# Feed-forward stages of a decoder layer: a first pair of chunks in seven block products

## The chip, the core and the metric

One core of a Trainium2 chip runs the whole layer as one program. The metric is the device time of one execution in microseconds (us). A change of 0.2% is 3.9 us here.

## The reference

A layer for 256 tokens of width 2048, everything in float32: a half-step SwiGLU feed-forward stage, a token mixer with two attention branches, and a second feed-forward stage, each followed by a LayerNorm on the residual sum.

```python
def _swiglu(x, w_gate, w_up, w_down):
    return (jax.nn.silu(x @ w_gate) * (x @ w_up)) @ w_down
...
h = _layer_norm(ALPHA * h + 0.5 * _swiglu(h, ffn1_w_gate[l], ffn1_w_up[l], ffn1_w_down[l]), ln1_g[l], ln1_b[l])
mix = _mixer(h, ...)
h = _layer_norm(ALPHA * h + mix, ln2_g[l], ln2_b[l])
h = _layer_norm(ALPHA * h + 0.5 * _swiglu(h, ffn2_w_gate[l], ffn2_w_up[l], ffn2_w_down[l]), ln3_g[l], ln3_b[l])
```

The gate and up matrices are 2048 x 5632 each. The change lies in `x @ w_gate` and `x @ w_up` of both feed-forward stages, in their first 512 columns of each matrix.

## The kernel before, in words

**Numbers in two parts.** Every float32 operand is split into a high part (a cast on ACT, L154) and a low part (source minus high part, on DVE, L155). A product is three matmuls (`triple`, L208 to L210): high x high, high x weights' low, low x weights' high. Each moves 512 columns. So no weight reaches TensorE before ACT and then DVE have gone over it. The two parts of a block of weights stand in a pair of tiles, `wring`, out of a ring of 10 pairs at first and of 6 in the steady state: this is how far ACT and DVE can work ahead of TensorE.

**Tiles and chunks.** The 256 tokens are two halves, b = 0 and 1. The 2048 rows of weights are 16 k tiles of 128; x is kept turned, in four quads of 4 k tiles (quad 0 holds k tiles 0 to 3). Gate and up are cut into 22 chunks of 512 columns (256 of gate, 256 of up). A unit is two k tiles of a chunk, one load of 512 KB: `raw` (4 buffers) when it is used once, `sraw` when it stays for several uses.

**Plain units and seven products.** `project` does a chunk plainly: 8 units, each used for both token halves, 12 matmuls a unit. `Hybrid.group` does a pair of chunks together. It takes the two token halves, the two chunks and two groups of k tiles as a 2 x 2 block product in Winograd's form, with seven products (forms 1 to 7, two units of 6 matmuls each) where eight would be needed. This holds for k tiles 0 to 7; the rest of the pair is plain. The weights' sums that the forms need are made in place in `sraw` blocks, by adds on DVE (L430) and by accumulating loads that POOL issues (L432). The sums of x are made once a stage by `Seven` (`fa`, `fb` at L289, split into `xs`; the negated quad at L313) and `Extra` (`fe`, `xe`, `xm`; L329, L341). The order of forms and plain units is a string (`"15pp6p7p2q4q3qq"`: digits are forms, p and q plain units of the first and second chunk).

**The opening of a stage.** Chunks 0 and 1 are done by `project`, one after the other: 16 units, 192 matmuls. x arrives quad by quad meanwhile: in the first stage by loads (`load_x`, L1453 to L1456), in the second from LayerNorm's rows, normalised (L895), transposed on TensorE (L673) and scaled (L680, L681 or ACT L685). The second token half's products run up to five units behind the first's (`lag`), since its x comes later. From chunks 2 and 3 on, the groups run; the first of them starts its banks unseeded, the later ones seeded (`begin`). In the second stage the blocks 11, 12 and 22 of the first group are loaded ahead, during chunk 1 (L979).

**Order.** Each engine runs its own queue in order. The order is fixed when the program is built: `later` puts a step some units on, `tc.issue_after` keeps an instruction behind another. Finished banks are taken by `half`: Silu on ACT (L914), product on DVE (L921, `hb`), turning (L717, `blocks`) and a store. A group's banks are first joined with a sum that was kept in SBUF (L940, `gus`; `snap` by ACT).

## Time and profile before

| what | us |
|---|---|
| three timed runs | 1965.83, 1966.58, 1967.08 |
| median | 1966.58 |
| span of the profiled execution, first to last instruction | 1963.9 |
| PE busy in it | 1952.0 |
| DVE busy | 1779.9 |
| ACT busy | 1251.5 |
| first stage's opening (first product to the first group) | about 5 to 50 |
| second stage's opening | about 1274 to 1318 |

The timed runs give the whole execution and the profile gives its span; about 2.7 us of the median lie outside the span. A row of a timeline has start, length, engine, line, operation, what it writes and reads, and in brackets the idle time ahead of it with what ended it. Overlapping instructions of an engine are pipelined: the distance of two starts is then the cost of one, not its length.

### The profile page before, as it was taken

How to read it: one execution, taken by the hardware profiler on the slowest of the kernel's cores; microseconds unless marked ns; L12 is line 12 of the kernel's file. 1: busy time of each engine (PE TensorE's matmuls, PEld its weight loads, DVE VectorE, ACT ScalarE, POOL GpSimd, SP SyncE). 2: the span in 40 equal slices, each digit the busy share in tenths (PEclk: the TensorE clock that was granted, in tenths of full speed). 3: DMA queues.
4: the chain of work that ended last, by engine and by line, in shares of the span. 5: the costliest groups of instructions: out<-in, count | busy, mean ns of one | idle time of the engine just before them, and what ended most of it. 6: DMA issues, size and time to landing. Idle time of an engine off the chain costs nothing.

```text
span 1963.9 us, 25802 instructions
## 1 busy us (share of the span) xinstructions
PE 1952.0 (99%) x8763; PEld 1617.7 (82%) x8763; DVE 1779.9 (91%) x2189; ACT 1251.5 (64%) x1640; POOL 312.1 (16%) x536
## 2 busy tenths in 40 slices
PE   9999999999999999999999999999999999999998
PEld 7888888888888898888788888888888888888886
DVE  7999999999998879988987777789999999999997
ACT  6666766676655566666667655556676666665662
POOL 0112111122100010102241530001211112210000
PEclk9999999999999999999999999999999999999999
DMA  8978888878776667767685798587888878787773
GB/s 314 289 225 262 270 260 249 257 233 300 272 235 222 210 216 258 239 223 252 211 254 195 237 305 271 201 264 254 252 269 263 250 240 277 241 318 236 277 232 124
DMA packets 150228, 488.86 MB, mean 249 GB/s; under 512 B 21792, under 2 KB 22096, under 8 KB 150096
## 3 DMA queue, kind: packets, MB, share of 16 engines
q1 hardware_dynamic: 119232, 401.00, 59.7%
q0 software_dynamic: 30720, 86.09, 16.8%
q8 instruction: 68, 1.11, 0.2%
q14 instruction: 64, 0.52, 0.1%
q10 hardware_dynamic: 144, 0.13, 0.0%
HBM read 456.73 MB, written 30.41 MB: 248 GB/s over the span
## 4 chain that ended last, share of the span: by engine, by line
PE 95%; DVE 2%; DMA 1%; issue 1%; ACT 0%; POOL 0%; SPq 0%; DVEq 0%; ACTq 0%; POOLq 0%
PE mm L208 30%; PE mm L210 30%; PE mm L209 30%; DVE wring L155 1%; PE tr L208 1%; PE tr L210 1%; PE tr L209 1%; PE tr L673 0%; DMA turned<-turn 0%; ACT wring L154 0%; DMA sraw<-in_wdk_dram 0%; DVE sraw L430 0%; PE tr L1376 0%; PE tr L1304 0%; PE tr L1378 0%
## 5 line engine op out<-in xcount | busy, mean ns | idle before, releaser
L154 ACT CAST wring<-raw 128x1024 fp32r<-128x1024 f32 (+2 forms) x468 | 482.7, 1035 | 323.5 <-PE mm L210 237.6
L155 DVE TENSOR_TENSOR wring<-raw,wring 128x1024 fp32r<-128x1024 f32 (+2 forms) x468 | 557.0, 1198 | 95.6 <-ACT wring L154 93.5
L154 ACT CAST wring<-sraw 128x1024 fp32r<-128x1024 f32 x436 | 453.1, 1052 | 201.7 <-DVE sraw L430 83.6
L155 DVE TENSOR_TENSOR wring<-sraw,wring 128x1024 fp32r<-128x1024 f32 x436 | 520.3, 1218 | 20.6 <-ACT wring L154 17.8
L208 PE MATMUL mm<-wring,h 128*128 128x512 f32 (+2 forms) x1248 | 480.9, 385 | 0.1
L210 PE MATMUL mm<-wring,h 128*128 128x512 f32 (+2 forms) x1248 | 480.3, 385 | 0.0
L209 PE MATMUL mm<-wring,h 128*128 128x512 f32 (+2 forms) x1248 | 479.9, 385 | 0.0
L208 PE MATMUL mm<-wring,xs 128*128 128x512 f32 x776 | 302.2, 389 | 0.5 <-ACT snap L387 0.5
L209 PE MATMUL mm<-wring,xs 128*128 128x512 f32 x776 | 302.1, 389 | 0.0
L210 PE MATMUL mm<-wring,xs 128*128 128x512 f32 x776 | 301.9, 389 | 0.0
L210 PEld LDWEIGHTS mm<-wring,h 128*128 128x128 f32 x1248 | 234.4, 188 | 47.0 <-DVE h L155 0.7
L208 PEld LDWEIGHTS mm<-wring,h 128*128 128x128 f32 x1248 | 234.4, 188 | 46.7 <-ACT h L154 0.6
L209 PEld LDWEIGHTS mm<-wring,h 128*128 128x128 f32 x1248 | 234.4, 188 | 46.1
L430 DVE TENSOR_TENSOR sraw<-sraw,sraw 128x1024 f32<-128x1024 f32 x168 | 199.1, 1217 | 2.0 <-DMA sraw<-in_wdk_dram 1.6
L208 PEld LDWEIGHTS mm<-wring,xs 128*128 128x128 f32 x776 | 145.6, 188 | 31.0 <-ACT snap L387 0.9
L209 PEld LDWEIGHTS mm<-wring,xs 128*128 128x128 f32 x776 | 145.7, 188 | 30.5 <-DVE wring L155 0.3
L210 PEld LDWEIGHTS mm<-wring,xs 128*128 128x128 f32 x776 | 145.7, 188 | 30.2
L719 POOL DMA_DIRECT2D hT<-blocks x176 | 96.8, 563 | 368.3 <-DVE blocks L717 367.2
L209 PE MATMUL mm<-wring,x 128*128 128x512 f32 x336 | 130.9, 390 | 0.2 <-DVE wring L155 0.2
L208 PE MATMUL mm<-wring,x 128*128 128x512 f32 x336 | 130.1, 390 | 0.8 <-ACT wring L154 0.8
L210 PE MATMUL mm<-wring,x 128*128 128x512 f32 x336 | 130.7, 389 | 0.0
L432 POOL DMA_DIRECT2D sraw<-in_gu_dram x40 | 35.6, 892 | 371.4 <-DVE sraw L430 334.5
(328 smaller groups left out, 2292.4 us busy)
## 6 DMA issues: line engine op xcount, KB each, us to landing
sraw<-in_gu_dram SPq DMA_DIRECT2D x160, 512.0 KB, 5.2
raw<-in_gu_dram SPq DMA_DIRECT2D x158, 512.0 KB, 5.0
raw<-in_dn_dram SPq DMA_DIRECT2D x140, 512.0 KB, 4.7
sraw<-in_gu_dram POOLq DMA_DIRECT2D x40, 512.0 KB, 7.5
sraw<-in_dn_dram SPq DMA_DIRECT2D x36, 512.0 KB, 5.4
eraw<-in_gu_dram SPq DMA_DIRECT2D x64, 256.0 KB, 5.8
raw<-in_w_out_dram SPq DMA_DIRECT2D x32, 512.0 KB, 4.3
hraw<-hT POOLq DMA_DIRECT2D x56, 256.0 KB, 5.9
```

The source lines that it names most:

```text
L154: cast[0] = S.copy(hi, src)
L155: lows[0] = V.tensor_tensor(out=lo, in0=src, in1=hi.bitcast(F32), op=ALU.subtract)
L208: PE.matmul(o, xh, wh, start=first, stop=False, skip_group_check=again)
L209: PE.matmul(o, xh, wl, start=False, stop=False, skip_group_check=again)
L210: PE.matmul(o, xl, wh, start=False, stop=last, skip_group_check=again)
L430: last = V.tensor_tensor(out=R[src][i], in0=R[src][i], in1=R[add[1]][i], op=ALU.add)
L432: nc.gpsimd.dma_start(R["12"][s], source("22", s), accum_op=ALU.add)
L719: nc.gpsimd.dma_start(to.rearrange("(g r) (i f) -> i r g f", g=4, i=4)[i], t[32 * i:32 * (i + 1), :].rearrange("r (g f) -> r g f", g=4))
```

## The change

Chunks 0 and 1 are now a pair too, in a new method `Hybrid.opening`, with the order `"pqpq1pq536qp742"`. K tiles 8 to 15 (quads 2 and 3) are plain and come first, 8 units of 12 matmuls. K tiles 0 to 7 (quads 0 and 1) are the block product, 14 units of 6 matmuls. So the opening has 22 units and 180 matmuls where it had 16 units and 192. x comes in the order of quads 2, 3, 0, 1, and quads 0 and 1 are no longer split for themselves (`formed`), only their sums are. Form 4 reads the block that forms 1, 5 and 6 have turned into a sum; two of the sums are made by accumulating loads on POOL (after form 1 and after form 6, two loads each), two by adds on DVE. The first group after it is seeded, and the loads ahead of the second stage are gone. The cut diff (in the order's rows below and in the new program all lines are shifted: L155 is L159, L430 is L565 in a group and L438 in the opening, L940 is L1069, L921 is L1056, L895 is L1030):

```diff
@@ class Acts
+            self.formed = formed
+            self.quads = [q for q in range(4) if q not in formed] + list(formed)
...
         def put(self, q, b, src, i0=0, n=4):
+            if q in self.formed:
+                return
@@ class Seven
+            self.opened = [self.minus] + self.steps[:4]
@@ class Hybrid
+        def opening(self, w0, w1, done, order, hook, guard, settle):
...
+            left = {b: 5 for b in "YWZX"}
+            blocks = {"11": (w0, 0), "21": (w0, 2), "22": (w1, 2)}
+            plan = {1: ("11", "11", None, "A"), 5: (None, "11", None, "D"), 6: (None, "11", "22", "A"),
+                    7: (None, "22", None, "A"), 2: ("21", "21", None, "Y"), 4: (None, "11", "21", "W"),
+                    3: ("22", "22", None, "Z")}
...
+                    done(n, m, banks[b], snap[key], op)
+            def plus(key, other):
+                V.tensor_tensor(out=snap[key], in0=snap[key], in1=snap[other], op=ALU.add)
...
+            def seventh(u, p, s):
...
+                    if add is not None:
+                        with behind_split(s + 1):
+                            last = V.tensor_tensor(out=t, in0=t, in1=R[add][s], op=ALU.add)
+                    pair = next_pair()
+                    with guard(u), tc.issue_after(last.ins) if last is not None else nullcontext():
+                        split_in_line(True, *pair, t)
+                    if p in (1, 6):
+                        nc.gpsimd.dma_start(R["11" if p == 1 else "22"][s], w1[s], accum_op=ALU.add)
...
@@ class LayerNorm
-            for c in range(4):
+            for c in self.x.quads:
@@ def ffn
-        project(wgu[0], x, KD, 512, lambda b, bank: gu_done(0, b, bank), hook=first_hook,
-                between=between, norm=norm)
-        project(wgu[1], x, KD, 512, lambda b, bank: gu_done(1, b, bank), hook=second, norm=norm, free=(0, 0))
-        look(3, 4)
-        hy = Hybrid(x, seven, KD, extra=extra, early=early)
+        formed = dict(zip((7, 9, 11, 13, 15, 18) if alone else (4, 8, 11, 13, 15, 18), seven.opened + [extra.make]))
+        hy.opening(wgu[0], wgu[1], lambda n, b, bank, snap, op: sum_done(n, b, bank, snap, op), "pqpq1pq536qp742",
+                   first, guard, settle)
+        hy.widened()
...
-                     1 < p < KF // 4 - 1, p > 1)
+                     1 < p < KF // 4 - 1, True)
@@ the loads of x in the first stage
-    def first_tokens(j):
-        if j % 2 == 0:
-            load_x(j // 2, 0)
-
-    def second_tokens(j):
-        if j % 2 == 0:
-            load_x(j // 2, 1)
+    def tokens(u, late):
+        for q, b in {(0, 0): ((2, 0),), (0, 1): ((2, 1),), (3, 0): ((0, 0),), (4, 0): ((3, 0),), (5, 0): ((3, 1),),
+                     (6, 0): ((0, 1), (1, 0), (1, 1))}.get((u, late), ()):
+            load_x(q, b)
```

**DVE, end of the first stage's opening.** The row before, from the last plain splits of chunk 1 (`raw_415` and on) over the first group's form 1 (`sraw_463`, `sraw_464`) to form 5 (the two L430 adds and the split behind them):

```order
L155 TENSOR_TENSOR wring_115<-raw_415,wring_114 128x1024
L155 TENSOR_TENSOR wring_105<-raw_431,wring_104 128x1024
L313 SCALAR_TENSOR_TENSOR xs_441<-xraw_123,xs_441 128x512
L155 TENSOR_TENSOR wring_103<-raw_444,wring_102 128x1024
L155 TENSOR_TENSOR wring_121<-sraw_463,wring_120 128x1024
L155 TENSOR_TENSOR wring_119<-sraw_464,wring_118 128x1024
L155 TENSOR_TENSOR wring_117<-raw_477,wring_116 128x1024
L430 TENSOR_TENSOR sraw_463<-sraw_463,sraw_465 128x1024
L430 TENSOR_TENSOR sraw_464<-sraw_464,sraw_466 128x1024
L155 TENSOR_TENSOR wring_115<-sraw_463,wring_114 128x1024
```

And now, from the last split of the opening (form 2's second unit) over form 1 (`wring_105`, `wring_103` from `sraw_214`, `sraw_215`) to the split of form 5 (`wring_121`) in the first group:

```order
L159 TENSOR_TENSOR wring_115<-sraw_375,wring_114 128x1024
L411 TENSOR_TENSOR snap_275<-snap_275,snap_274 128x512
L1069 TENSOR_TENSOR gus_449<-mm_169,snap_275 128x512
L159 TENSOR_TENSOR wring_105<-sraw_214,wring_104 128x1024
L1056 TENSOR_TENSOR hb_453<-gus_449,sg_451 128x256
L1069 TENSOR_TENSOR gus_474<-mm_148,snap_274 128x512
L159 TENSOR_TENSOR wring_103<-sraw_215,wring_102 128x1024
L1056 TENSOR_TENSOR hb_453<-gus_474,sg_476 128x256
L565 TENSOR_TENSOR sraw_214<-sraw_214,sraw_404 128x1024
L565 TENSOR_TENSOR sraw_215<-sraw_215,sraw_405 128x1024
L1069 TENSOR_TENSOR gus_500<-mm_136,snap_275 128x512
L159 TENSOR_TENSOR wring_121<-sraw_214,wring_120 128x1024
```

Three plain splits and the negated quad of x (`xs`) stood ahead of form 1 before, with two adds and one plain split up to form 5. Now the opening's sums (`snap`), the joining of all four banks (`gus`) and three of their products (`hb`) stand between the splits.

**DVE, the second stage, behind the normalised rows of the second token half.** Here `h2raw` and `full` are scaled quads of x, `h` their split parts, `fe` and `fa` sums of them. The row before, from the scaling of quad 1 (`h2raw_10289`) to the first sum of x (`fa`):

```order
L680 TENSOR_TENSOR h2raw_10289<-tr_10387,cols_9667 128x512
L155 TENSOR_TENSOR wring_119<-raw_10523,wring_118 128x1024
L155 TENSOR_TENSOR h_1511_10383<-h2raw_10274,h_1510_10382 128x512
L681 TENSOR_TENSOR h2raw_10289<-h2raw_10289,cols_9667 128x512
L680 TENSOR_TENSOR full_10416<-tr_10411,cols_9667 128x512
L155 TENSOR_TENSOR h_1515_10407<-h2raw_10300,h_1514_10406 128x512
L155 TENSOR_TENSOR h_1511_10383<-h2raw_10289,h_1510_10382 128x512
L681 TENSOR_TENSOR full_10416<-full_10416,cols_9667 128x512
L329 TENSOR_TENSOR fe_10490<-h2raw_10300 128x128 x2
L329 TENSOR_TENSOR fe_10490<-h2raw_10300,fe_10490 128x128 x2
L155 TENSOR_TENSOR h_1515_10407<-full_10416,h_1514_10406 128x512
L289 TENSOR_TENSOR fa_10517<-h2raw_10274,h2raw_10289 128x512
```

And now, from the scaling of quad 3 (`full_10386`) to the first unit of form 1 (`wring_10138`):

```order
L815 TENSOR_TENSOR full_10386<-tr_10381,cols_9667 128x512
L334 TENSOR_TENSOR fe_10606<-h2raw_10274 128x128
L816 TENSOR_TENSOR full_10386<-full_10386,cols_9667 128x512
L334 TENSOR_TENSOR fe_10606<-h2raw_10274 128x128
L334 TENSOR_TENSOR fe_10606<-h2raw_10274,fe_10606 128x128
L159 TENSOR_TENSOR h_1496_10377<-h2raw_10274,h_1495_10376 128x512
L159 TENSOR_TENSOR h_1496_10377<-full_10386,h_1495_10376 128x512
L815 TENSOR_TENSOR h2raw_10311<-tr_10402,cols_9667 128x512
L334 TENSOR_TENSOR fe_10606<-h2raw_10274,fe_10606 128x128
L816 TENSOR_TENSOR h2raw_10311<-h2raw_10311,cols_9667 128x512
L318 SCALAR_TENSOR_TENSOR xs_10452<-h2raw_10300,xs_10452 128x512
L159 TENSOR_TENSOR wring_10138<-sraw_10455,wring_10137 128x1024
```

Before, only the splits of x and the first sums stand here, and one split of weights (`wring_119`) is early among them. Now the low part of the negated quad 0 (`xs_10452`, form 1's x) and the split of form 1's weights stand behind all the scaling of quads 3 and 1.

## Prediction

> **What bounds the kernel now.** I read the page first, then the waits of PE, then the windows around the two openings, then DVE's timeline there. The page's first lines and its chain:

> ```profile
> span 1963.9 us, 25802 instructions
> PE 1952.0 (99%) x8763; PEld 1617.7 (82%) x8763; DVE 1779.9 (91%) x2189; ACT 1251.5 (64%) x1640; POOL 312.1 (16%) x536
> ...
> PE 95%; DVE 2%; DMA 1%; issue 1%; ACT 0%; POOL 0%; SPq 0%; DVEq 0%; ACTq 0%; POOLq 0%
> ```

> The waits of PE (who, for whom: us in total, times, longest) hold 6 us in all, and 4.1 of them at the very end:

> ```profile
> PE tr L869 <- ACT pair L867: 4.1, 1, 4.1
> ...
> PE mm L208 <- ACT wring L154: 0.8, 1, 0.8
> PE mm L208 <- ACT snap L387: 0.5, 1, 0.5
> ```

> So TensorE sets the end, and a matmul that goes saves its own pitch, if nothing else comes late. The windows (stretch, its length, then busy us and count for PE, PEld, DVE, ACT, POOL, then the granted clock, DMA share, GB/s) give the pitch and show who is next: the first row is the steady state, the others hold the two openings.

> ```profile
> 60.00:600.00 540.00, 540.00 (x2384) 447.11 (x2384) 526.08 (x621) 361.55 (x455) 91.59 (x152) 1.00 0.81 260
> 4.00:50.00 46.00, 45.01 (x202) 36.80 (x202) 39.15 (x48) 31.48 (x40) 1.16 (x2) 1.00 0.91 330
> 1274.00:1320.00 46.00, 46.00 (x211) 37.77 (x210) 41.24 (x59) 27.45 (x40) 4.11 (x6) 1.00 0.77 263
> ```

> 540 us for 2384 matmuls is 0.2265 us each; I use 0.227. In the steady groups DVE is 97% busy: it is as near to its limit as TensorE. Only the openings leave it air (39 of 46 us, 41 of 46). The change takes matmuls out of the openings and puts DVE work into them, so the question is whether DVE's queue still runs ahead.

> **What is saved.** 180 matmuls for 192 in each opening: 24 x 0.227 = 5.4 us, 2.7 a stage.

> **What DVE gets, first opening.** DVE's timeline before, some rows:

> ```profile
> 12.00 1.29 DVE L155 TENSOR_TENSOR x<-xraw,x 128x512 fp32r<-128x512 f32 x2
> ...
> 28.27 2.35 DVE L155 TENSOR_TENSOR wring<-raw,wring 128x1024 fp32r<-128x1024 f32 x2
> 30.54 0.75 DVE L921 TENSOR_TENSOR hb<-mm,sg 128x256 f32<-128x256 f32 x2
> ...
> 38.62 1.22 DVE L155 TENSOR_TENSOR wring<-raw,wring 128x1024 fp32r<-128x1024 f32 x1
> ...
> 43.30 2.50 DVE L155 TENSOR_TENSOR wring<-sraw,wring 128x1024 fp32r<-128x1024 f32 x2 [3.47 <-ACT wring L154]
> ...
> 46.86 2.35 DVE L430 TENSOR_TENSOR sraw<-sraw,sraw 128x1024 f32<-128x1024 f32 x2
> ```

> Two wide instructions back to back take 2.35 and the next starts 0.08 before their end: 1.135 us a wide one (split or add). In the same way 0.605 for 128x512 and 0.335 for an `hb`. After 38.62 DVE was done with the opening and sat idle for 3.47 us: that was the lead. A check of these pitches on the old queue: from 12.00 on it holds 16 wide, 12 half-wide, 2 `hb` and five small ones (0.2 each), 18.2 + 7.3 + 0.7 + 1.0 = 27.2; with 0.5 of gaps its end is 39.7, and the trace has 38.62 + 1.22 = 39.84.

> The first five loads are the same size and order as before, so the new queue also gets to its x splits at 12.00. From there to the end of the split of form 5's first unit in the first group (the last order row but none of the block shown above) I count 31 wide ones (19 splits of the opening, 3 splits of x's sums, 4 adds, then form 1's two splits, two adds and form 5's split), 14 half-wide (2 splits of x, the negated quad, 4 sums of x, `xe`, 2 sums of `snap`, 4 `gus`), 3 `hb` and one small: 35.2 + 8.5 + 1.0 + 0.2 = 44.9. So without a single gap it ends at 12.0 + 44.9 + 0.1 = 57.0.

> TensorE wants that split at its 196th matmul. It has not waited since 7.75, so the 196th stands in the trace of before:

> ```profile
> 7.75 0.50 PE L209 MATMUL mm<-wring,x 128*128 128x512 f32 x1 [0.22 <-DVE wring L155]
> ...
> 51.22 0.39 PE L208 MATMUL mm<-wring,x 128*128 128x512 f32 x1
> ```

> At 51.2, then, against 57.0: TensorE must lose 5.8 us, whichever of its matmuls show it. This comes from the queue's length alone. Four sources of idle time add to it.

> - *A load in the way.* Quad 0 of x (256 KB) now stands ahead of the fourth unit's load. ACT's cast of that unit began as the load came:

> ```profile
> 12.39 1.05 ACT L154 CAST wring<-raw 128x1024 fp32r<-128x1024 f32 x1 [0.53 <-DMA raw<-in_gu_dram]
> ```

> At 0.40 MB/us 256 KB take 0.65, and the cast ends at 14.1 where DVE would be free at 13.2. With 0.1 more at form 1: 1.0 us.
> - *Two accumulating loads on the chain.* Form 5's split needs block 11 with block 12 added by POOL's load, issued once form 1's split has read it; form 7's needs the one that follows the last reader of block 22. How long such loads take, by the rows of their line:

> ```profile
> DMA to landing us min/median/max: 5.0/7.1/11.8
> ```

> The DMA issues (tile, queue, count, KB each, median us to landing), over the whole run and then in the first 75 us alone:

> ```profile
> sraw<-in_gu_dram SPq DMA_DIRECT2D x160, 512.0 KB, 5.2
> ...
> sraw<-in_gu_dram POOLq DMA_DIRECT2D x2, 512.0 KB, 10.4
> ```

> Between form 1's first split and form 5's DVE has, in the queue, one split, 4 sums of x, 4 wide ones: about 7.0 us after the split's end; a load of L with ACT's cast of 1.05 makes DVE wait L - 5.9. For the second pair, 6.5 us of work stand between: L - 5.4. I take 7.1, the median of all of them, as the two early ones (10.4) are few: 1.2 + 1.7 us. At 5.0 both waits vanish; at 10.4 they are 4.5 + 5.0.
> - *A reload.* The first group's form 1 takes block 11 anew, and its load must wait for form 4's split, with form 2's two splits, `hb`, a sum and a `gus` (4.9 us) between. 5.2 + 1.05 - 4.9 = 1.4 us; nothing, if the load is quick.

> First opening: 5.8 + 1.0 + 2.9 + 1.4 = 11.1 us of waiting less 2.7 = **+8.4**; +4.1 with quick loads.

> **Second opening.** The timeline's rows of DVE, then of PE, around LayerNorm's end:

> ```profile
> 1263.43 0.69 DVE L836 TENSOR_TENSOR z<-mm,z 128x512 f32<-128x512 f32 x1 [1.77 <-PE mm L210]
> ...
> 1266.26 1.92 DVE L895 TENSOR_SCALAR z<-z,mv,f 128x512 f32<-128x512 f32 x4
> 1269.76 0.69 DVE L155 TENSOR_TENSOR h<-h2raw,h 128x512 fp32r<-128x512 f32 x1 [1.59 <-ACT h L154]
> ...
> 1266.90 1.57 PE L673 MATMUL tr<-ident,z 128*128 128x128 f32 x12
> 1268.22 0.48 PE L208 MATMUL mm<-wring,y 128*128 128x512 f32 x1
> ...
> 1273.74 0.39 PE L208 MATMUL mm<-wring,h 128*128 128x512 f32 x1
> ```

> The first half's chain is as before; the first product stays at 1273.74. The second half's sum can enter DVE after 4 half-wide and 2 wide ones from 1269.76, at 1274.5, and takes what the first half's took (1263.43 to 1268.18, 4.75): 1279.2. The 18 matmuls of the first half cover this until 1277.8 and its first transposes can start there, so little is lost. Then the rows shown in the change: 7 half-wide and 4 small, 5.0, put form 1's first split at 1284.2, and TensorE wants it 32 matmuls and 16 transposes behind 1273.74, 7.3 + 1.8, at about 1283: a first wait of 1 to 2 us. From there to form 5 of the first group: 29 wide, 10 half-wide, 3 `hb`, 1 small = 40.2, so 1324.4. TensorE comes there after 195 matmuls (44.3) and 16 transposes (1.7; the 12 above took 1268.22 - 1266.90): 1319.7. Lost 4.7, with the same waits for loads (1.2 + 1.7 + 1.4) 9.0, less 2.7: **+6.3**; +2.0 with quick loads.

> ACT (31.5 and 27.5 busy of 46) gets 6 casts, 4 `snap` copies and loses 4 to 8 half casts: not a bound, and its casts lie beside DVE's other work. LayerNorm's order of quads only renames which rows come first, at no cost. The new POOL loads stand ahead of no store that anyone waits for in the opening, and SP's loads for later units are needed more than 5 us after they can be issued: nothing. Later groups: DVE has its lead back by the first group's end (its forms 2 to 4 need less of it), so the delay is not repeated and not regained either, since TensorE has no idle time to give back.

> **The sum.** 1963.9 + 8.4 + 6.3 = 1978.6 of span; the median of the runs lies 2.7 above the span: 1966.6 + 14.7 = **1981.3 us**.

> [...]

> **The rivals.**

> *A. Covered (faster).* The interleaved order lets TensorE do first matmuls of four units ahead of their low parts, and the ring of 6 pairs hides DVE's length, as it does in the steady groups. Then only the saving is left: 1966.6 - 5.4 = 1961.2. For it: in the steady state DVE at 97% never stops PE. Against it: a ring can lend only what was stored, and DVE starts with nothing. It decides at one point: whether form 5's split in the first group is through by 51.2, that is 5.8 us earlier than the queue allows. Chance 0.10.

> *B. Loads at their busy price (still slower).* The first opening's loads meet a DMA share of 0.91; at 10.4 for all, 3.3 more on each of four waits: 1981.3 + 13.2 = 1994.5. Chance 0.14.

> *C. Nearly even.* Quick loads and a lead that is regained in part (DVE's pitches a little shorter where it waits less): 1966.6 + 0 to 4. Chance 0.10.

> That it does not do what it says can be excluded: PE's queue is 24 rows shorter.

> **Numbers.** Forecast (1972 to 1990) 0.66, A 0.10, B 0.14, C 0.10. The bounds with all loads quick or all slow are 1972.7 and 1994.5; the range takes in C from its lower end, 1966.6, and leaves out A. A difference under 0.2% (3.9 us) is about what a measurement of this kernel cannot tell from none. Faster 0.10 (A), same 0.10 (C), slower 0.80 (the rest).

> **What would show it.** Right: PE's waits in 15 to 62 and about 1282 to 1330 sum to some 11 and 9 us, for `wring` by DVE; DVE without gaps there but behind accumulating loads; the split for the first group's form 5 ending near 62; everything later shifted, not changed. Wrong: PE without waits in both openings, or waits that go back to ACT or to a bank, or a shift that shrinks later.

## The result, and the profile after

The changed kernel takes 1995.8 us (median of four runs, 1995.5 to 1996.8) against 1966.7 before: 1.0151 times the time before, 95% interval 1.0137 to 1.0166, 29 us slower where 14.7 were forecast. The sign and the engine were right, the size forecast was half of what came. The page's first lines and its chain:

```profile
span 1993.7 us, 25789 instructions
...
PE 1963.8 (99%) x8739; PEld 1617.7 (81%) x8739; DVE 1805.0 (91%) x2211; ACT 1263.7 (63%) x1652; POOL 318.7 (16%) x544
...
PE 90%; DVE 4%; DMA 3%; issue 1%; ACT 1%; POOL 0%; SPq 0%; DVEq 0%; ACTq 0%; POOLq 0%
```

The 24 matmuls are gone from PE's count, and 25 us of DVE's busy time have come. The chain shows who holds the end now: DVE 4% and DMA 3%, where they had 2 and 1. The waits of PE that were not there before (who, for whom: us in total, times, longest):

```profile
PE mm L213 <- DVE wring L159: 10.2, 14, 1.3
PE mm L212 <- ACT wring L158: 4.6, 7, 1.2
```

L213 is the matmul with a pair's low part (DVE's), L212 the one with its high part (ACT's). The windows of the first opening (columns as in the prediction):

```profile
26.00:29.00 3.00, 1.33 (x5) 0.55 (x3) 1.17 (x1) 1.04 (x1) 0.00 (x0) 1.00 1.05 274
29.00:33.00 4.00, 3.88 (x10) 3.08 (x11) 0.36 (x2) 1.38 (x2) 0.00 (x0) 0.58 0.96 357
33.00:40.00 7.00, 5.40 (x21) 3.45 (x20) 6.79 (x7) 7.00 (x11) 0.00 (x0) 1.00 0.03 12
54.00:74.00 20.00, 14.31 (x54) 9.01 (x52) 17.28 (x21) 12.40 (x16) 1.69 (x2) 1.00 0.79 245
74.00:600.00 526.00, 526.00 (x2322) 435.53 (x2322) 513.78 (x590) 350.75 (x441) 89.38 (x148) 1.00 0.81 257
```

From 74 on all is as before: the loss is made in the opening and its first group, and never regained. Inside there are three pictures: TensorE idle with DVE idle too (26 to 29, DMA busy), TensorE at a granted clock of 0.58 (29 to 33), and TensorE idle with DVE full (33 to 40, DMA at 0.03). DVE's timeline shows its gaps:

```profile
12.53 1.28 DVE L159 TENSOR_TENSOR x<-xraw,x 128x512 fp32r<-128x512 f32 x2
14.69 1.22 DVE L159 TENSOR_TENSOR wring<-raw,wring 128x1024 fp32r<-128x1024 f32 x1 [0.88 <-ACT wring L158]
...
27.84 1.23 DVE L159 TENSOR_TENSOR wring<-sraw,wring 128x1024 fp32r<-128x1024 f32 x1 [2.71 <-ACT wring L158]
32.70 1.23 DVE L159 TENSOR_TENSOR wring<-sraw,wring 128x1024 fp32r<-128x1024 f32 x1 [3.64 <-ACT wring L158]
...
47.39 1.23 DVE L159 TENSOR_TENSOR wring<-sraw,wring 128x1024 fp32r<-128x1024 f32 x1 [1.01 <-ACT wring L158]
49.75 1.22 DVE L159 TENSOR_TENSOR wring<-sraw,wring 128x1024 fp32r<-128x1024 f32 x1 [1.13 <-ACT wring L158]
...
57.50 3.50 DVE L159 TENSOR_TENSOR wring<-sraw,wring 128x1024 fp32r<-128x1024 f32 x3 [1.46 <-ACT wring L158]
...
63.47 1.23 DVE L159 TENSOR_TENSOR wring<-sraw,wring 128x1024 fp32r<-128x1024 f32 x1 [1.15 <-ACT wring L158]
...
70.06 2.36 DVE L159 TENSOR_TENSOR wring<-sraw,wring 128x1024 fp32r<-128x1024 f32 x2
```

The last row is the prediction's landmark, the split for form 5 of the first group: its first unit ends at 70.06 + 1.14 = 71.2, where TensorE wanted it at 51.2. 20.0 us late, less the 2.7 saved, is 17.3; the first transpose of the first stage's LayerNorm, at 683.0 in the trace before, indeed comes 17.7 later. In the second stage the landmark (1349.46 below) ends at 1350.6. The rows around LayerNorm's end stand 17.15 later than before (1280.58 for 1263.43), so that is 1333.5 on the old clock for a wanted 1319.7: 13.8.

Every gap says "ACT wring", so the cause lies in what ACT waited for. ACT's and POOL's timelines at the six gaps from 27.84 on:

```profile
18.19 1.02 POOL L443 DMA_DIRECT2D sraw<-in_gu_dram  x1 [16.08 <-DVE wring L159]
19.50 0.86 POOL L443 DMA_DIRECT2D sraw<-in_gu_dram  x1 [0.28 <-DVE wring L159]
40.43 0.84 POOL L443 DMA_DIRECT2D sraw<-in_gu_dram  x1 [20.07 <-ACT wring L158]
41.57 0.85 POOL L443 DMA_DIRECT2D sraw<-in_gu_dram  x1 [0.29 <-issue]
...
26.76 1.04 ACT L158 CAST wring<-sraw 128x1024 fp32r<-128x1024 f32 x1 [3.74 <-DMA sraw<-in_gu_dram]
31.62 1.04 ACT L158 CAST wring<-sraw 128x1024 fp32r<-128x1024 f32 x1 [3.82 <-DMA sraw<-in_gu_dram]
46.31 1.05 ACT L158 CAST wring<-sraw 128x1024 fp32r<-128x1024 f32 x1 [4.19 <-DMA sraw<-in_gu_dram]
48.66 1.05 ACT L158 CAST wring<-sraw 128x1024 fp32r<-128x1024 f32 x1 [1.31 <-DMA sraw<-in_gu_dram]
...
53.87 1.28 ACT L1048 ACT_TABLE_LOAD   x1
61.45 1.05 ACT L158 CAST wring<-raw 128x1024 fp32r<-128x1024 f32 x1 [3.50 <-PE mm L214]
```

Issue to cast: 8.6, 12.1, 5.9 and 7.1 us for the four accumulating loads, and 2.71 + 3.64 + 1.01 + 1.13 = 8.5 us of DVE's idle time behind them. The gap at 57.50 stands behind ACT's table load for Silu (1.28 us), the one at 63.47 behind a cast that waits until TensorE gives a pair of the ring back.

The second opening, from the row that places it on the old clock, by DVE's gaps and ACT's rows at the first of them:

```profile
1280.58 0.69 DVE L971 TENSOR_TENSOR z<-mm,z 128x512 f32<-128x512 f32 x1 [1.77 <-PE mm L214]
...
1308.55 1.23 DVE L159 TENSOR_TENSOR xs<-fa,xs 128x1024 fp32r<-128x1024 f32 x1 [2.35 <-ACT xs L158]
1310.57 1.22 DVE L159 TENSOR_TENSOR wring<-raw,wring 128x1024 fp32r<-128x1024 f32 x1 [0.79 <-ACT wring L158]
...
1326.86 1.22 DVE L159 TENSOR_TENSOR wring<-sraw,wring 128x1024 fp32r<-128x1024 f32 x1 [0.51 <-ACT wring L158]
1329.38 1.23 DVE L159 TENSOR_TENSOR wring<-sraw,wring 128x1024 fp32r<-128x1024 f32 x1 [1.29 <-ACT wring L158]
...
1349.46 1.23 DVE L159 TENSOR_TENSOR wring<-sraw,wring 128x1024 fp32r<-128x1024 f32 x1 [1.41 <-ACT wring L158]
...
1306.99 0.59 ACT L418 COPY snap<-mm 128x512 f32<-128x512 f32 x1 [4.94 <-PE mm L214]
1307.47 1.05 ACT L158 CAST xs<-fa 128x1024 fp32r<-128x1024 f32 x1
...
1347.90 0.58 ACT L535 ACTIVATE mm<-mm 128x512 f32<-128x512 f32 x1 [2.00 <-PE mm L214]
```

Here the accumulating loads cost only 0.51 + 1.29. The large gap is another: ACT stands 4.9 us at form 1's copy into `snap`, which waits for form 1's last matmul, and x's cast, which DVE needs, queues behind it. The gap of 1.41 at the landmark stands behind another such wait, the seeding of the first group's bank (L535). Both matmuls that ACT waited for come right behind a stretch at half the clock (granted clock 0.50 from 1302.82 to 1306.23 and from 1343.78 to 1347.19), so these two gaps are ACT's order and the clock together. The last stretch of waits of PE in the second stage, with what follows:

```profile
1350.74 0.80 PE L213 MATMUL mm<-wring,xs 128*128 128x512 f32 x1 [0.53 <-DVE wring L159]
1351.34 0.63 PE L214 MATMUL mm<-wring,xs 128*128 128x512 f32 x1
1351.76 0.63 PE L212 MATMUL mm<-wring,xs 128*128 128x512 f32 x1
...
1353.89 0.46 PE L214 MATMUL mm<-wring,xs 128*128 128x512 f32 x1
```

From 1350.74 to 1353.89 seven matmuls take 3.15 us, 0.43 apart in the middle, where 7 x 0.227 = 1.6 is their time: half the clock (granted clock 0.50 from 1350.60 to 1354.02). TensorE waits no more after it, so these 1.6 us are lost whole, and 13.8 + 1.6 - 2.7 = 12.7 is what the second stage lost. The 13.8 hold two more pieces of the clock: form 1's and the one ahead of L535.

### The profile page after: what moved, and what is told of

The parts are those of the page before. It is cut to its first block, busy times and chain, and to the rows that moved or that the text cites. A ratio compares the mean times of both kernels' runs of the same rounds, so it can differ in the third digit from the quotient of the medians.

```text
span 1993.7 us, 25789 instructions
## 1 busy us (share of the span) xinstructions
PE 1963.8 (99%) x8739; PEld 1617.7 (81%) x8739; DVE 1805.0 (91%) x2211; ACT 1263.7 (63%) x1652; POOL 318.7 (16%) x544
## 4 chain that ended last, share of the span: by engine, by line
PE 90%; DVE 4%; DMA 3%; issue 1%; ACT 1%; POOL 0%; SPq 0%; DVEq 0%; ACTq 0%; POOLq 0%
PE mm L213 29%; PE mm L214 29%; PE mm L212 29%; DVE wring L159 2%; DMA sraw<-in_gu_dram 1%; ACT wring L158 1%; PE tr L213 1%; PE tr L214 1%; PE tr L212 1%; DMA raw<-in_gu_dram 1%; DMA sraw<-in_wdk_dram 1%; DVE sraw L565 0%; PE tr L808 0%; DVE sraw L438 0%; DMA sraw<-in_wdv_dram 0%
## 5 line engine op out<-in xcount | busy, mean ns | idle before, releaser
L158 ACT CAST wring<-raw 128x1024 fp32r<-128x1024 f32 (+2 forms) x452 | 466.4, 1035 | 337.3 <-PE mm L214 255.6
L159 DVE TENSOR_TENSOR wring<-raw,wring 128x1024 fp32r<-128x1024 f32 (+2 forms) x452 | 537.9, 1198 | 88.9 <-ACT wring L158 86.4
L158 ACT CAST wring<-sraw 128x1024 fp32r<-128x1024 f32 x464 | 480.3, 1052 | 202.4 <-DVE sraw L565 77.3
L159 DVE TENSOR_TENSOR wring<-sraw,wring 128x1024 fp32r<-128x1024 f32 x464 | 553.3, 1218 | 32.1 <-ACT wring L158 29.9
L212 PE MATMUL mm<-wring,h 128*128 128x512 f32 (+2 forms) x1216 | 468.2, 385 | 0.8 <-ACT mm L535 0.7
L214 PE MATMUL mm<-wring,h 128*128 128x512 f32 (+2 forms) x1216 | 467.9, 385 | 0.0
L213 PE MATMUL mm<-wring,h 128*128 128x512 f32 (+2 forms) x1216 | 467.2, 384 | 0.0
L213 PE MATMUL mm<-wring,xs 128*128 128x512 f32 x824 | 324.7, 394 | 9.0 <-DVE wring L159 9.0
L212 PE MATMUL mm<-wring,xs 128*128 128x512 f32 x824 | 324.0, 394 | 5.0 <-ACT wring L158 4.1
L214 PE MATMUL mm<-wring,xs 128*128 128x512 f32 x824 | 323.3, 392 | 0.0
L212 PEld LDWEIGHTS mm<-wring,h 128*128 128x128 f32 x1216 | 228.4, 188 | 46.4 <-ACT mm L535 1.2
L214 PEld LDWEIGHTS mm<-wring,h 128*128 128x128 f32 x1216 | 228.4, 188 | 45.4 <-DVE h L159 0.5
L213 PEld LDWEIGHTS mm<-wring,h 128*128 128x128 f32 x1216 | 228.5, 188 | 44.7
L565 DVE TENSOR_TENSOR sraw<-sraw,sraw 128x1024 f32<-128x1024 f32 x168 | 199.2, 1218 | 0.8 <-DMA sraw<-in_wdk_dram 0.6
L213 PEld LDWEIGHTS mm<-wring,xs 128*128 128x128 f32 x824 | 156.3, 190 | 46.6 <-DVE wring L159 14.3
L212 PEld LDWEIGHTS mm<-wring,xs 128*128 128x128 f32 x824 | 156.1, 189 | 40.9 <-ACT wring L158 7.1
L214 PEld LDWEIGHTS mm<-wring,xs 128*128 128x128 f32 x824 | 156.1, 189 | 32.2
L213 PE MATMUL mm<-wring,x 128*128 128x512 f32 x304 | 119.2, 392 | 1.2 <-DVE wring L159 1.2
L212 PE MATMUL mm<-wring,x 128*128 128x512 f32 x304 | 118.6, 392 | 1.4 <-ACT mm L535 0.7
L214 PE MATMUL mm<-wring,x 128*128 128x512 f32 x304 | 118.7, 390 | 0.0
## 6 DMA issues: line engine op xcount, KB each, us to landing
sraw<-in_gu_dram SPq DMA_DIRECT2D x172, 512.0 KB, 5.3
raw<-in_gu_dram SPq DMA_DIRECT2D x142, 512.0 KB, 4.8
raw<-in_dn_dram SPq DMA_DIRECT2D x140, 512.0 KB, 4.7
sraw<-in_gu_dram POOLq DMA_DIRECT2D x48, 512.0 KB, 7.0
sraw<-in_dn_dram SPq DMA_DIRECT2D x36, 512.0 KB, 5.9
raw<-in_w_out_dram SPq DMA_DIRECT2D x32, 512.0 KB, 4.5
```

What stands on the lines that cost most here:

```text
L158: cast[0] = S.copy(hi, src)
L159: lows[0] = V.tensor_tensor(out=lo, in0=src, in1=hi.bitcast(F32), op=ALU.subtract)
L212: PE.matmul(o, xh, wh, start=first, stop=False, skip_group_check=again)
L213: PE.matmul(o, xh, wl, start=False, stop=False, skip_group_check=again)
L214: PE.matmul(o, xl, wh, start=False, stop=last, skip_group_check=again)
L565: last = V.tensor_tensor(out=R[src][i], in0=R[src][i], in1=R[add[1]][i], op=ALU.add)
```

## The experiments

All times stand beside the kernel before on the same chip (1965.7 to 1967.0); where the text says "less", it is the difference of two medians as they stand, and runs of one kernel lay up to 4 us apart (e3: 1983.3 and 1987.4, the profile is of the latter). For each run's profile the table splits the delay of its span: up to the first transpose of the first stage's LayerNorm (683.0 before), and from the first transpose of the second stage's (1266.9 before) on; what lies between is the mixer, which moved by up to 2.7 by itself, so the first stage's share of one run is good to 2 or 3 us; the second stage's came out at 0.2 and 0.1 where that stage is unchanged (e1, e12).

| kernel | us | first stage | second stage |
|---|---|---|---|
| changed kernel | 1995.8 | 17.7 | 12.7 |
| e1 first stage only | 1985.1 | 18.6 | 0.2 |
| e2 second stage only | 1977.1 | -0.3 | 10.2 |
| e3 no accumulating loads | 1985.3 | 10.3 | 10.0 |
| e4 no adds by DVE | 1983.2 | 10.0 | 6.8 |
| e5 filled | 1993.7 | 19.7 | 8.2 |
| e6 copy of x | 1991.7 | 18.5 | 8.0 |
| e7 block 12 plainly | 1995.5 | 13.4 | 12.7 |
| e8 adds on POOL | 1993.1 | 15.8 | 11.4 |
| e9 form 3 first | 2001.0 | 18.9 | 15.9 |
| e10 Silu early | 1993.3 | 17.2 | 11.2 |
| e11 both of these | 2000.7 | 17.8 | 16.1 |
| e12 before, with 12 adds | 1978.4 | 12.6 | 0.1 |
| e13 filled, second only | 1992.8 | 17.8 | 9.0 |
| e14 filled elsewhere | 1994.5 | 19.4 | 10.2 |
| e15 what gained, together | 1988.3 | 10.7 | 10.7 |

**One stage at a time.** Theory: the stages add up, and DVE's chain with its gaps sets each. Rivals: DVE's length alone, TensorE's clock, or loads alone.

```diff
+NEW = (1,)        # (2,) in e2
+        paired = n in NEW
+        if paired:
             hy.opening(...)
+        else:
+            project(wgu[0], ...); project(wgu[1], ...)
```

> The change in the first stage alone; the second stage opens as in the kernel before. Two stages that don't touch each other (theory): the trace of the changed kernel is about 17 us late behind its first opening, so 1983 to 1985 us. The prediction's own term for this stage was +8.4: 1975. If the delay of one stage were partly given back later, less than 1980.

> The change in the second stage alone. Theory: the rest of the 29 us, about 12 to 13, so 1978 to 1980 us. The prediction's own term for this stage was +6.3: 1973.

Measured: 19.4 and 11.4 us above the kernel before. They sum to 30.8 for 29.1 together: to within 1.7 us the stages are independent, and nothing is given back. e2 lost 10.2 in the second stage where the changed kernel lost 12.7, with the same instructions: its trace has the half clock behind form 1 only, and not the two later stretches (mean granted clock of the run 0.998 for 0.994), and its landmark comes 1.4 us earlier behind the stage's first transpose. So the two stretches were worth about 2.5 us.

**Loads and adds left out.**

```diff
-                    if p in (1, 6):                       # e3
-                        nc.gpsimd.dma_start(R["11" if p == 1 else "22"][s], w1[s], accum_op=ALU.add)
...
-                            last = V.tensor_tensor(out=t, in0=t, in1=R[add][s], op=ALU.add)     # e4
```

> Both openings without their accumulating loads: block 12 is never added to blocks 11 and 22, so the output of those chunks is another one; all else is kept. Theory (each split behind such a load stands on the chain of DVE, which sat idle 8.5 us for four of them in the first opening): 8 to 9 us less for each stage, 1977 to 1981 us, and the gaps of DVE there gone. Rival (DVE's queue is late by its own length, the gaps only come where it has time): within 4 us of 1996. Rival (the half granted clock behind the gaps is what costs): the 7 us of half clock go too, down to 1972.

> Both openings without the four adds that DVE makes in blocks 11 and 22 (the splits read the blocks as they are, so the sums are left out and the output is another one); the accumulating loads stay. Theory (DVE's queue, gaps and all, sets the end): 4 x 1.14 us for each stage, about 9 in all, 1986 to 1988 us. Rival (the loads alone set the pace, DVE's work lies beside them): within 3 us of 1996.

Without the loads 10.4 us went, not 17. The first stage gave 7.4, and its landmark says why, in DVE's timeline:

```profile
24.30 2.35 DVE L159 TENSOR_TENSOR wring<-sraw,wring 128x1024 fp32r<-128x1024 f32 x2
...
48.73 3.50 DVE L159 TENSOR_TENSOR wring<-sraw,wring 128x1024 fp32r<-128x1024 f32 x3 [1.46 <-ACT wring L158]
...
61.28 2.36 DVE L159 TENSOR_TENSOR wring<-sraw,wring 128x1024 fp32r<-128x1024 f32 x2
```

Form 5's splits at 24.30 have no gap, and the landmark starts at 61.28 for 70.06, 8.8 earlier. Of this, 1.2 stood already at x's splits (11.34 for 12.53), ahead of any such load, and three small gaps of DVE are new (0.68, 0.55 and 0.51): the 8.5 us count nearly one for one. Only 7.4 of the 8.8 reach LayerNorm, since here a stretch at half clock follows the landmark (62.51 to 65.92). The second stage gave 2.7: my expectation had carried the first stage's gaps over, against the rows above (1.8). The gap of 1.46 behind the table load is there unchanged, so it is not the loads'. Without the adds 12.6 us went, more than their 9.1: in the first stage the gaps that stood at 57.50 and 63.47 are gone ahead of the landmark. My reading, not tried by itself, is that an add stands between two casts of ACT, so it costs its length and the turn DVE, ACT, DVE. Neither "only DVE's length" nor "only the loads" holds.

**More work for TensorE.**

```diff
+    FILL1 = {(5, 0): (4, 3), (5, 1): (0, 1), (3, 0): (0, 4), (6, 0): (2, 5)}
+    FILL2 = {(1, 0): (5, 3)}            # e13: FILL1 = {};  e14: FILL2 = {(6, 0): (5, 0), (6, 1): (3, 0)}
...
+                    for _ in range(n):
+                        last = PE.matmul(o, hi[:, 0, :], hi.rearrange("p k t -> p (k t)"), start=True, stop=True)
```

> 27 more matmuls (a quad of x by itself, into a bank that nobody reads), put where TensorE waits in the openings and then ran at the half clock: 4 and 3 at form 5's first unit, 1 and 6 to 7 more at forms 5, 3 and 6 in the first stage, 5 and 3 at form 1 in the second. 6.1 us of work for TensorE. Theory (DVE's chain sets how late the opening ends, TensorE's idle time and its half clock lie in its shadow): within 2.5 us of 1996, with the half clock gone from 29 to 33 and 43 to 47. Rival (the half clock is itself on the path): three stretches of about 8 matmuls at 0.2 us more are saved, 4 to 5 us less, 1991. Rival (TensorE's work sets the end): 6 us more, 2002.

> Only the eight extra matmuls at form 1 of the second stage (5 ahead of its first matmul, 3 behind), 1.8 us of work for TensorE; the first stage is that of the changed kernel. Theory (the half clock behind the two waits there delays form 1, its copy on ACT, x's cast behind it and so DVE): as in the run with fillers in both stages, 4 to 5 us less in the second stage, 1991 to 1992 us, and no half clock from 1300 to 1355. Rival (that run's gain was only where its instructions fell): within 1.5 us of 1996.

> The same eight matmuls ahead of form 6 of the second stage, where TensorE does not wait in the changed kernel: the control. Theory (only the clock counts): no gain, 1996 to 1998 us, and the half clock behind form 1's waits stays. Rival (any shift of TensorE's queue there gains): 1991 to 1993.

27 matmuls more and 2.1 us less: TensorE's own work in the openings is free, and saving 24 matmuls there could bring nothing while DVE is late. That rules out "TensorE's work sets the end", and the half clock is gone from 29 to 33 and from 43 to 47 (granted clock 1.00 in both). With the second stage's eight alone 3.0 us went (runs from 1991.5 to 1994.1) and no half clock is left in that stage (granted clock 1.00 from 1295 to 1308 and from 1340 to 1355); with the control 1.3 (1992.8 to 1996.2), and the two ranges overlap. But the control did not keep the half clock. Its own rows of PE, at the place where the changed kernel fell to half:

```profile
1304.42 0.50 PE L460 MATMUL mm<-wring,xs 128*128 128x512 f32 x1 [1.21 <-ACT wring L158]
...
1305.86 0.50 PE L462 MATMUL mm<-wring,xs 128*128 128x512 f32 x1 [0.71 <-DVE wring L159]
1306.20 0.39 PE L463 MATMUL mm<-wring,xs 128*128 128x512 f32 x1
1306.43 0.40 PE L214 MATMUL mm<-wring,xs 128*128 128x512 f32 x1
```

The same two waits (1.21 and 0.71 for 1.19 and 0.70), and the full clock behind them, 0.23 apart. The traces show where the two differ. The stretches at half clock begin at multiples of 3.413 us from one another (in the changed kernel at 29.65, 43.30, 1302.82, 1343.78 and 1350.60) and each is 3.41 us long: one slice of a grid. The slice ahead of the fall in the changed kernel, and then the two slices of the control (its grid laid by its own stretches at half clock), columns as before:

```profile
1299.41:1302.82 3.41, 1.52 (x6) 0.64 (x5) 3.41 (x6) 2.64 (x4) 0.00 (x0) 1.00 0.97 368
...
1300.28:1303.69 3.41, 2.93 (x15) 2.16 (x14) 3.41 (x9) 3.41 (x9) 0.57 (x2) 1.00 0.96 279
1303.69:1307.11 3.42, 1.98 (x7) 1.35 (x8) 3.42 (x5) 1.62 (x2) 0.75 (x1) 1.00 0.97 393
```

In the changed kernel both waits lie in one slice, of which TensorE is busy 1.52 us; in the control the border falls into the first wait, and the slices hold 2.93 and 1.98. The half clock followed the slice of 1.52 and neither of the other two. The border lay 1.67 us behind the end of the first wait in the changed kernel and 0.73 ahead of it in the control, so the same pair of waits had the half clock behind it in one run and not in the other, and the control isn't one. e5, with a half clock in one place only (mean granted clock of the run 0.997 for 0.994), is still 26.7 slower than the kernel before: most of the loss doesn't need it.

**The copy on ACT.**

```diff
-                S.copy(snap[...], banks["D" if p == 5 else "A"])
+                S.copy(snap[...], self.x.raws[0][:, 0, :] if p == 1 else banks["D" if p == 5 else "A"])
```

> The copy of form 1's bank into snap, on ACT, takes a quad of x instead of the bank, so that it waits for no matmul (the sums with it are other ones). Theory (in the second stage ACT stood 4.9 us behind this copy and held up x's cast, so that DVE sat idle 2.4 and 0.8 us): 2 to 3 us less, 1993 to 1994 us, all of it in the second stage. Rival (another wait takes its place): within 1 us of 1996.

4.1 us less, all in the second stage (8.0 for 12.7); DVE's gap at `xs` fell from 2.35 to 0.4. But form 1 ran at the full clock in this run (mean granted clock of the run 0.997 for 0.994), and that is part of it. Two runs with the copy as it was and the full clock there (e10 and the control) have a gap of 0.78 at `xs`, not 2.35. The first split for form 7 comes 42.8 us behind the stage's first transpose in the changed kernel, 41.8 and 42.0 in those two, 40.9 here: about 1 us is the clock's, and about 1 us the copy's, less than the 2 to 3 expected.

**Adds moved.**

```diff
+            blocks = {..., "12": (w1, 0)}                                             # e7
+            5: ("12", "11", "12", "D"), 7: (None, "22", "12", "A")                    # e7
...
-                            last = V.tensor_tensor(out=t, in0=t, in1=R[add][s], op=ALU.add)
+                        GP.tensor_tensor(out=t, in0=t, in1=R[add][s], op=ALU.add)     # e8
```

> Block 12 is loaded plainly once for each opening and added by DVE to blocks 11 and 22 in place of the accumulating loads; the output stays the reference's. Four more adds of 1.14 us for DVE in each stage. Theory by the gaps that stood behind such loads (8.5 us in the first opening, 1.8 in the second): -8.5 + 4.5 and -1.8 + 4.5, so about 1.3 us less, 1993 to 1996 us. Rival (as the run without the accumulating loads saved 10.4 in all): 10.4 less 9.1, the same number, but then with equal shares in both stages. Rival (a load's landing matters, DVE's work does not): 1985.

> The four adds of the opening that DVE made (blocks 11 and 22) go to POOL, which is idle there; the output stays the reference's. No trace so far shows what such an add takes on POOL. Theory (DVE's queue sets the end): if POOL takes under 2.5 us for one, near the run that left these adds out, 1984 to 1987 us. If an add on POOL takes 5 us or more, the splits behind it wait for it: 1996 or later.

Block 12 by plain loads and DVE, with the accumulating loads left out as in e3: the same time, with 4.3 us less in the first stage and nothing in the second. The gaps had said -4.0 and +2.7, within what a share is good to; it speaks against equal shares, but not strongly. The adds on POOL took 2.4 to 3.5 us, and only 2.7 us went in all. POOL's row and DVE's beside it:

```profile
33.54 2.39 POOL L437 TENSOR_TENSOR sraw<-sraw,sraw 128x1024 f32<-128x1024 f32 x1 [2.63 <-DVE wring L159]
...
33.67 3.34 DVE L159 TENSOR_TENSOR xs<-fb,xs 128x1024 fp32r<-128x1024 f32 x1 [0.21 <-ACT xs L158]
```

A split of 1.22 us took 3.34 and ended at 37.01, 1.08 behind POOL's add: the add was moved off DVE's queue and still stood in DVE's way.

**Order and table.**

```diff
-        "pqpq1pq536qp742"
+        "pqpq1pq356qp742"                                                  # e9
...
-            self.opened = [self.minus] + self.steps[:4]
+            self.opened = [self.minus, self.sums, self.steps[2], self.steps[1], self.as_is]   # e9
...
+            if u == (8 if alone else 9):                                   # e10
+                S.activation(sm(1), zero[:, 0:1], AF.Silu)
```

> Form 3 ahead of forms 5 and 6 in both openings (and x's sums for it first), so that two splits of DVE, 2.3 us, stand between form 1 and form 5, which waits for the accumulating loads; the output stays the reference's. Theory (the gaps behind these loads count one for one): the 6.4 us of DVE's idle time ahead of form 5 in the first opening fall to about 4, and little changes in the second: 1993 to 1994 us. Rival (the loads land later still, as other loads come in between): 1996.

> One Silu of a column of zeros on ACT ahead of form 5, so that ACT loads its table there and not between the casts of the first group; the output stays the reference's. Theory (the 1.28 us table load stands in the chain of casts, and DVE sat idle 1.5 us behind it in the first stage, 0.5 in the second): 1 to 2 us less, 1994 to 1995 us. Rival (another wait takes its place): 1996.

> Both of the other two edits of this set together, the best version that the findings so far give with the output kept. Theory: the sum of the two, 1991 to 1993 us, still 24 to 26 above the kernel before, as DVE's longer queue stays.

Form 3 first made it worse, 2001.0. DVE's gap moved to form 3 and grew, and the queues of POOL and ACT show why:

```profile
17.01 1.02 POOL L443 DMA_DIRECT2D sraw<-in_gu_dram  x1 [14.90 <-DVE wring L159]
...
27.06 1.99 ACT L158 CAST wring<-sraw 128x1024 fp32r<-128x1024 f32 x2 [6.34 <-DMA sraw<-in_gu_dram]
...
29.08 1.23 DVE L159 TENSOR_TENSOR wring<-sraw,wring 128x1024 fp32r<-128x1024 f32 x1 [6.40 <-ACT wring L158]
```

ACT's row at 27.06 is two casts. The first is form 5's, by the semaphore that it waits on, that of the accumulating load issued at 17.01, which lands at 26.96. The second, at 28.01, is form 3's, whose plain load had landed at 20.84; DVE's split at 29.08 follows it. So the edit put form 3 first on DVE, but on ACT form 5's cast still stood ahead of it and waited for its load: the two splits that were to fill DVE's wait for this load stood behind the load themselves. In the second stage both of form 5's casts stand ahead on ACT, and DVE's gap is 7.78. Neither theory had that, and the edit as built doesn't test whether two splits ahead of form 5 would help. The early Silu did what was expected: the gap of 1.46 fell to 0.17, 2.4 us less in all (1 to 2 expected), of which about 1 may be the clock at form 1. Both together are as slow as e9, 2000.7 where 1991 to 1993 were expected.

**DVE's work alone, in the kernel before.**

```diff
+            if norm is None and j < 6:
+                for _ in range(2):
+                    lows[0] = V.tensor_tensor(out=early["load"], in0=..., in1=..., op=ALU.add)
```

> The kernel before with 12 adds of 128x1024 more on DVE (x's quads, into a tile that nobody reads) behind the splits of chunk 1 in the first stage: 13.6 us for DVE and nothing else. Theory (DVE's queue may be late by its idle time and its smallest lead, and each us beyond that is TensorE's): idle time 3.5 and 1.2, smallest lead of a low part 2.9 near 60 us, so 13.6 - 7.6 = 6.0 us more, 1972 to 1974 us. Rival (the ring of pairs and later groups take it up): 1967.

13.6 us of work for DVE, and 12.2 more, where idle time and lead were to take up 7.6. A stretch of half clock behind the last wait (12 matmuls at 0.43) is 2.4 of the 12.2; without it 9.8 remain, so 3.8 were taken up. DVE's and ACT's rows behind the adds:

```profile
70.12 2.36 DVE L155 TENSOR_TENSOR wring<-sraw,wring 128x1024 fp32r<-128x1024 f32 x2 [4.63 <-ACT wring L154]
...
44.52 1.06 ACT L154 CAST wring<-raw 128x1024 fp32r<-128x1024 f32 x1 [4.59 <-DMA raw<-in_gu_dram]
67.62 1.04 ACT L154 CAST wring<-sraw 128x1024 fp32r<-128x1024 f32 x1 [5.01 <-DMA sraw<-in_gu_dram]
```

DVE's idle time is only in part a reserve. What it waits for (a `raw` load whose buffer its own splits free, an accumulating load issued behind its own split) moves back with it, so the gap comes again later, 4.63 us here.

**The best with the output kept.**

> What gained with the output kept, put together: block 12 plainly loaded and added by DVE in the first stage (4.3 us less there), the eight matmuls at form 1 and an early Silu in the second (4.5 and 1.5 less). Theory (the parts add up): 10.3 us less, 1985 to 1987 us, still 18 to 20 above the kernel before. Rival (the last two share one wait): 1988.

1988.3 us: 7.5 less than the changed kernel, not 10.3, so the parts do not quite add up, and still 21 above the kernel before (1.0108 times it, 1.0091 to 1.0124). No version here beats that kernel.

## Why the prediction was half right

The first stage lost 17.7 for the +8.4 forecast, the second 12.7 for +6.3.

- *What bounds the kernel; the saving.* Right. 24 matmuls went, and TensorE's work in the openings turned out free (e5), so the saving only counts against the lateness.
- *DVE's queue in the first opening.* Right. 44.9 us of work from 12.0 were counted to the landmark. It is 58.7 from 12.53 to 71.2, less 12.2 of gaps: 46.5, so 1.6 longer than counted and 0.5 later at its start.
- *Two accumulating loads on the chain: 2.9 us.* This is the term that failed in the first stage. It measured 8.5 in the first opening (6.35 for the 1.2 at form 5, 2.14 for the 1.7 at form 7), 1.8 in the second. I took the median over the run, 7.1, though the two early loads of the trace before, 10.4, lay in the very stretch; they took 8.6 and 12.1. I also counted one wait for each pair of loads, though the second of a pair lands later and waits again. e3 showed it: without the loads these gaps were gone and the landmark came 8.8 us earlier.
- *A load in the way, 1.0.* Right: 0.88. *A reload, 1.4*: a gap of 1.46 came in that place, but it is the table load's (e10), and it stayed when the accumulating loads went.
- *ACT is not a bound, its casts lie beside DVE's other work.* This step failed in both stages. ACT has time to spare, but its queue runs in order: a copy that waits 4.9 us for a matmul holds x's cast, and with it DVE for 2.35 + 0.79 us; about 1 us of that is the copy's own (e6) and about 1 the clock's. A table load does the same for 1.5 (e10), a cast that waits for a pair of the ring for 1.15 in each stage, and the seeding of the first group's bank (L535), which waits for a matmul, for 1.41 in the second, where that matmul came behind a stretch at half clock; these last two are read in the traces, not tried alone.
- *The second opening, +6.3.* 12.7 in the changed kernel, 10.2 in e2, 8.2 and 9.0 in e5 and e13, which have eight matmuls more and no half clock in that stage. The landmark came at 1333.5 on the old clock, forecast 1324.4 + 4.3: the gaps were 8.3 us for 4.3.
- *TensorE's clock.* The prediction had no term for it, so it stood at nothing. In the second stage I estimate it from the rows at 1.6 behind the last wait, about 1.4 at L535 (DVE's gap) and about 1 at form 1, some 4 of the 6.4 us missed there; the two later ones are borne out by e2 (2.5 us), the first by e6, e10 and the control. The rest, about 2.4, is ACT's queue and the small terms.
- *Later groups.* Right: shifted, not changed.
- *Rival B* (1994.5, loads at 10.4) came close to the time, but not for its reason: its waits came true in the first opening alone, and the rest was ACT's queue and the clock: the nearness is luck. *Rival A* was wrong where it was said to be: the landmark was 20 us late.
- *The signs.* Waits of PE of some 11 and 9 us were named, and 11.6 (15 to 75) and 7.3 (1299 to 1353) came, yet twice the time went: the listed waits hold neither the half clock nor the slower start behind each wait (0.34 for 0.23 to the next matmul). So that agreement is luck too. DVE without gaps but behind accumulating loads did not come: 1.46 and 1.15 stand behind a table load and the ring.

The sum of the first stage is closed: 20.0 - 2.7 = 17.3 for 17.7 measured. That of the second closes with the 1.6. Its share for the half clock at form 1 is good to some tenths only, and a run in which nothing but the clock differs was not made.

## What to carry to other kernels

Where a second engine is 97% busy behind the first, price a saving on the first by what it adds to the second's queue, up to the first landmark at which the first must have the second's result. Then go through the in-order queues that feed that engine: for each instruction that waits for something far away (a copy of a result, an accumulating load, a table load, a load into a buffer not yet free), ask what stands behind it. Idle time of the late engine is a reserve only if what it waits for doesn't hang on that engine itself. And waits of the first engine can cost more than their length: in the changed kernel five slices of 3.41 us in which TensorE sat idle for 1.5 to 1.9 us were each followed by a slice at half the clock, 1.6 us more at the one that no later wait hides.
